# Gate slabs of the second half in pairs, by seven block products in place of eight

## The chip, the cores and the metric

The kernel runs on 1 core of one Trainium2 chip. The metric is the device time of one execution in microseconds. Before the change it is 2825.84 us, the median of 3 runs (2825.59 to 2826.05).

## What is computed

One inference step of a one-layer encoder with two branches, on 2048 prompt rows and 64 sample rows of width 1024, in float32. Cut to the parts that matter here:

```python
h = rmsnorm(x, norm_g)
q, k, v, ga, u, gb, mg = split(h @ w_in)        # six parts of 1024 columns, mg of 2048
att = stick_breaking(q, k, v)                   # 8 heads of 128, strictly causal
p   = trailing_mean(u, windows 2, 4, 8, 16) - u # 4 groups of 256 channels
pb  = (p @ w_pool[group]) * pool_scale
y_a = (att * silu(ga)) @ w_br_a
y_b = (pb  * silu(gb)) @ w_br_b
m   = sigmoid(mg[:, :1024]) * y_a + sigmoid(mg[:, 1024:]) * y_b
y   = rmsnorm(x + m @ w_out, final_g)
```

The sample attends to 4096 cached keys too. New keys, values and the last pooling rows are outputs as well.

## The kernel before

**Products.** Every float32 operand is split exactly into two parts of at most 12 significant bits, `hi` and `lo` (function `split`: a cast on ScalarE, then a subtraction on VectorE). One product of two operands is three matmuls: hi·hi, lo·hi, hi·lo. A contraction over 1024 is eight tiles of 128, so 24 matmuls per block of one PSUM bank.

**Halves.** The rows are worked off in two halves: first prompt rows 0 to 1023 with the 64 sample rows, then prompt rows 1024 to 2047. `hhi` and `hlo` hold the transposed, normalised rows of the half at hand. A *slab* is 128 columns of `w_in`: `proj` loads it (two transfers of 256 KB into `raw`, three buffers), splits it into `whi` and `wlo` (two buffers each), and multiplies it with the half's row blocks (`GROUPS_B`: two blocks of 512 rows in the second half). 48 matmuls make one slab there. An `evac` function then takes the bank.

**Stages of a half.** The heads: projections of a head beside the attention of the head before it. The attention's tail, with gate slabs beside it. Pooling groups (`pool_group`: two slabs of u, window sums on VectorE, a split, and a map of 12 matmuls per block that is deferred, `mapped`) and the other gate slabs: 8 *branch gates* (silu of gb) and 16 *merge gates* (sigmoid of mg). In the first half the attention of the sample runs beside the last two.

A branch gate is stored to DRAM as `gb_d`, loaded again when the pooling needs it (`gbl`), multiplied into the pooled map and stored as `bT_d`. Merge gates are stored to `sm_d`, attention results to `aT_d`.

**Closing.** `load_weight` brings a 1024 x 1024 weight in 16 tiles (`wraw`, split into `bwhi` and `bwlo`), `load_rows` eight row tiles (`rraw`, into `rhi` and `rlo`). `branch` then multiplies, in five blocks of up to 424 rows and eight channel tiles each, first for y_a, then for y_b; the last stage multiplies with w_out. For the first of these, rows and weights are loaded while 15 merge slabs of the second half run, through two raw buffers:

```python
rawp = [wside, 2]
...
raw = rawp[0].tile([P, 512], F32, name="wraw", bufs=rawp[1])
...
early = chain(load_weight(w_br_a[0], wa), load_rows(aT_d, *POST[0], wside, rows0))
run((chain(*[proj(GROUPS_B, [merge_gate(1, c)]) for c in range(1, 2 * KT)]), 15 * slab_ns(1)), (early, 30.0))
```

**What sets the order.** TensorE runs in the order in which the program is traced. `run` takes several generators of steps and traces them spread evenly over one another; `defer` puts a function off by some time, and `settle(True)` traces all that is still put off. On the other engines and on SP, which issues all of these transfers, a scheduler sets the order when the program is built; each then runs strictly in that order.

Of the kernel before, what the change touches and what calls it, by code (L numbers as in the profile page):

```python
# [15 lines left out]
P = 128  # L16
# [16 lines left out]
# rows of a half, as the columns of its transposed operand: blocks of one PSUM bank  # L33
# [4 lines left out]
# rows of the closing phases: prompt 0..1023, sample, prompt 1024..2047  # L38
# [5 lines left out]
def kernel(  # L44
# [18 lines left out]
    gb_d = dram.tile([D, R], F32, name="gb_d")  # L63
# [10 lines left out]
    def split(hi, lo, src, eng=None):  # L74
        """src = hi + lo exactly, each part of at most 12 significant bits."""
        if eng == "v":
            nc.vector.tensor_copy(hi, src)
        else:
            nc.scalar.copy(hi, src)  # L79
        (nc.gpsimd if eng == "g" else nc.vector).tensor_tensor(lo, src, hi.bitcast(F32), op=ALU.subtract)  # L80
# [12 lines left out]
    # row tiles: half A holds prompt rows 0..1023 and the sample, half B the other prompt rows  # L93
# [21 lines left out]
    def run(*gens):  # L115
        """Trace the generators' steps, spread evenly over one another: (generator, its time in ns)"""
# [26 lines left out]
    with ExitStack() as front:  # L143
# [13 lines left out]
        # of the sample's new keys, for two heads: NEG where key >= query; and the identity of 64, twice  # L157
# [104 lines left out]
        def load_w(src, kts, width, eng=None):  # L262
            """src [kts * 128, width] -> hi, lo [128, kts, width]"""
# [33 lines left out]
        def gate_evac(half, dst, row, silu):  # L297
            def evac(g, c0, n, ps):
                s = outgoing("sgm")
                nc.scalar.activation(s[:, 0:n], ps[:, 0:n], AF.Sigmoid)  # L300
                if silu:
                    nc.vector.tensor_tensor(s[:, 0:n], ps[:, 0:n], s[:, 0:n], op=ALU.mult)
                r0 = half * RA + c0
                nc.sync.dma_start(dst[row:row + P, r0:r0 + n], s[:, 0:n])
            return evac

        def merge_gate(half, c):
            return (OFF_M + c * P, gate_evac(half, sm_d, c * P, False))

        def branch_gate(half, c):  # L310
            return (OFF_GB + c * P, gate_evac(half, gb_d, c * P, True))

# [1 line left out]
        def pool_group(half, gi):  # L314
            w = WINDOWS[gi]
            groups = groups_of(half)
            parts, gates = {}, {}
# [7 lines left out]
            def pooled(hi, lo, t0, n, ext, start):  # L325
                """rows whose u lies at columns BUF.. of ext, after its predecessors"""
# [17 lines left out]
            def evac_u(s):  # L344
                c = gi * 2 + s

                def evac(g, c0, n, ps):
# [22 lines left out]
                    if s == 1:  # L370
                        for t in range(2):
                            row, r0 = (gi * 2 + t) * P, half * RA + c0
                            gates[t, g] = attp.tile([P, 528], F32, name="gbl", tag="be", bufs=8)
                            nc.sync.dma_start(gates[t, g][:, 0:n], gb_d[row:row + P, r0:r0 + n])
# [4 lines left out]
            def mapped(g, c0, n, s):  # L379
# [4 lines left out]
                for k in range(2):  # L384
# [10 lines left out]
            # the maps of a block follow the next block's first products  # L395
# [41 lines left out]
        # q, k, gate (transposed) and v (by rows) of the sample  # L437
# [13 lines left out]
        def natural(src, rows, dst):  # L451
            """src [128, rows] transposed to rows, stored at dst [rows, 128]; returns the tile"""
# [12 lines left out]
        def head_proj(half, hd, fine=False):  # L465
# [10 lines left out]
            def spill(kind, c, o, src):  # L476
                """k (transposed) or v (by rows) of the first half's rows, for the second half"""
# [79 lines left out]
        def strictly_causal(t, fill):  # L557
            """t [128 queries, 128 keys]: fill where key >= query"""
# [3 lines left out]
        def weights_of_block(z, off, carry, diag=False, be=None):  # L562
            """z [128, keys] at columns off.. (in PSUM, or in be) -> break weights, and the stick that is left"""
# [23 lines left out]
        class Stream:  # L587
            """The attention of a half's prompt rows: scores of tile n, transposes of tile n - 4,
            products with the values of tile n - 5."""
# [72 lines left out]
            def steps(self, hd):  # L662
                """up to the last score of a head (None: to the end)"""
# [12 lines left out]
        def sample_stream():  # L676
# [5 lines left out]
            def keys(n):  # L682
# [3 lines left out]
                if c == NEW:  # L686
# [7 lines left out]
                    # [hi, lo], [lo, hi]; [hi, 0], [0, hi]  # L694
# [27 lines left out]
            def scores(n):  # L722
# [7 lines left out]
                # each head's bank: the products of q_hi in the head's own rows, that of q_lo in the others  # L730
# [30 lines left out]
            def transposes(n):  # L761
# [7 lines left out]
                # [key, key tile, head, part, query]  # L769
# [289 lines left out]
```

## Time and profile before

| | |
|---|---|
| median of 3 runs | 2825.84 us |
| span of the profiled execution, first to last instruction | 2823.3 us |
| TensorE busy (matmuls) | 2771.4 us, 98% |
| VectorE (DVE) busy | 1678.2 us, 59% |
| ScalarE (ACT) busy | 1194.2 us, 42% |
| GpSimd (POOL) busy | 447.9 us, 16% |
| moved by DMA | 307.83 MB, 109 GB/s on average |
| heads of the first half | until about 570 us |
| attention's tail, sample, pooling and gates of the first half | about 570 to 1110 us |
| heads of the second half | about 1110 to 1820 us |
| attention's tail with four branch gates, second half | about 1820 to 1925 us |
| pooling and the other gates, second half | about 1925 to 2260 us |
| closing phases | from 2260.4 us |

The profile is one execution. Its span runs from the first to the last instruction; the time of a run is some 2.5 us longer. Matmuls are pipelined, so the length of a matmul row is more than the spacing of two matmuls, and TensorE can count as busy in a small gap. In a row of the timeline the first number is the start, the second the length; in brackets stands the idle time of the engine before it and what ended it. In a row of waits stand the waiting engine and tile, what it waited for, the total, the number of waits and the longest. In a row of a stretch stand its bounds and length, the busy time and number of instructions of TensorE, its weight loads, VectorE, ScalarE and GpSimd, then the granted clock of TensorE, the busy share of the DMA engines and GB/s.

### The profile page before, as it was taken

How to read it: one execution, taken by the hardware profiler on the slowest of the kernel's cores; microseconds unless marked ns; L12 is line 12 of the kernel's file. 1: busy time of each engine (PE TensorE's matmuls, PEld its weight loads, DVE VectorE, ACT ScalarE, POOL GpSimd, SP SyncE). 2: the span in 40 equal slices, each digit the busy share in tenths (PEclk: the TensorE clock that was granted, in tenths of full speed). 3: DMA queues.
4: the chain of work that ended last, by engine and by line, in shares of the span. 5: the costliest groups of instructions: out<-in, count | busy, mean ns of one | idle time of the engine just before them, and what ended most of it. 6: DMA issues, size and time to landing. Idle time of an engine off the chain costs nothing.

```text
span 2823.3 us, 42058 instructions
## 1 busy us (share of the span) xinstructions
PE 2771.4 (98%) x15044; PEld 2415.1 (86%) x15044; DVE 1678.2 (59%) x2847; ACT 1194.2 (42%) x2500; POOL 447.9 (16%) x1107
## 2 busy tenths in 40 slices
PE   6999999999999999999999999999999999999998
PEld 5988898889998988888888888887778899999877
DVE  6555555577768683578887888885442022434543
ACT  4445444455555553455555555553223111211221
POOL 2112222220000002233343334330000000000000
PEclk9999999999999999999999999999999999999999
DMA  4223222234444454211111111113344264666432
GB/s 148 73 87 125 71 71 71 84 106 157 151 149 149 155 164 127 72 46 49 57 53 46 49 57 53 34 57 98 116 127 148 75 210 142 214 193 199 162 130 88
DMA packets 333309, 307.83 MB, mean 109 GB/s; under 512 B 30302, under 2 KB 288078, under 8 KB 333100
## 3 DMA queue, kind: packets, MB, share of 16 engines
q1 hardware_dynamic: 333100, 305.15, 34.4%
q8 instruction: 118, 1.93, 0.3%
q14 instruction: 91, 0.75, 0.1%
HBM read 208.99 MB, written 96.07 MB: 108 GB/s over the span
## 4 chain that ended last, share of the span: by engine, by line
PE 93%; DVE 4%; ACT 1%; DMA 1%; issue 1%; POOL 0%; SPq 0%; DVEq 0%; ACTq 0%; POOLq 0%
PE pj L282 17%; PE pj L284 17%; PE pj L283 17%; PE ps L952 4%; PE ps L953 4%; PE ps L954 4%; PE tr L636 4%; PE att L653 2%; PE att L652 2%; PE att L651 2%; PE ps L1015 2%; PE z L625 2%; PE ps L1016 2%; PE ps L1014 2%; PE z L624 2%; PE z L623 2%
## 5 line engine op out<-in xcount | busy, mean ns | idle before, releaser
L282 PE MATMUL pj<-hhi,whi 128*128 128x512 f32 (+2 forms) x2608 | 945.2, 362 | 0.0
L284 PE MATMUL pj<-hhi,wlo 128*128 128x512 f32 (+2 forms) x2608 | 917.9, 352 | 0.5 <-DVE wlo L80 0.5
L283 PE MATMUL pj<-hlo,whi 128*128 128x512 f32 (+2 forms) x2608 | 916.8, 352 | 0.1
L284 PEld LDWEIGHTS pj<-hhi,wlo 128*128 128x128 f32 x2608 | 491.9, 189 | 65.9 <-DVE wlo L80 1.0
L282 PEld LDWEIGHTS pj<-hhi,whi 128*128 128x128 f32 x2608 | 494.4, 190 | 59.6 <-ACT sgm L300 0.4
L283 PEld LDWEIGHTS pj<-hlo,whi 128*128 128x128 f32 x2608 | 493.4, 189 | 58.8 <-DVE hlo L80 0.4
L577 DVE TENSOR_TENSOR_SCAN om<-om 128x513 f32<-128x513 f32 (+3 forms) x356 | 388.0, 1090 | 212.5 <-POOL om L559 108.2
L567 ACT ACTIVATE om<-z 128x512 f32<-128x512 f32 (+2 forms) x320 | 171.3, 535 | 323.0 <-PE z L625 273.9
L80 DVE TENSOR_TENSOR wlo<-raw,whi 128x512 fp32r<-128x512 f32 x248 | 171.6, 696 | 199.8 <-ACT whi L79 198.8
L580 DVE TENSOR_TENSOR be<-be,om 128x512 f32<-128x512 f32 (+3 forms) x356 | 230.4, 647 | 31.4
L79 ACT CAST whi<-raw 128x512 fp32r<-128x512 f32 x256 | 158.1, 623 | 171.4 <-PE pj L283 154.0
L79 ACT CAST a<-tr 128x512 fp32r<-128x512 f32 (+2 forms) x356 | 188.1, 528 | 100.4 <-PE tr L636 89.7
L80 DVE TENSOR_TENSOR a<-tr,a 128x512 fp32r<-128x512 f32 (+2 forms) x356 | 215.8, 607 | 23.8 <-ACT a L79 21.7
L952 PE MATMUL ps<-rhi,bwhi 128*128 128x424 f32 (+1 forms) x640 | 226.7, 354 | 0.8 <-issue 0.8
L953 PE MATMUL ps<-rlo,bwhi 128*128 128x424 f32 (+1 forms) x640 | 226.8, 354 | 0.0
L954 PE MATMUL ps<-rhi,bwlo 128*128 128x424 f32 (+1 forms) x640 | 226.3, 354 | 0.0
L579 POOL COPY carry<-om 128x1 f32<-128x1 f32 x356 | 77.9, 219 | 921.7 <-DVE om L577 881.2
L79 ACT CAST rhi<-rraw 128x424 fp32r<-128x424 f32 (+4 forms) x128 | 66.3, 523 | 293.2 <-PE ps L954 221.6
L956 DVE TENSOR_TENSOR bo<-ps,sg 128x424 f32<-128x424 f32 (+1 forms) x80 | 47.8, 597 | 228.7 <-PE ps L954 216.3
L636 PE MATMUL tr<-ident,be 128*128 128x128 f32 x1088 | 176.0, 274 | 6.1 <-DVE be L580 3.6
L636 PEld LDWEIGHTS tr<-ident,be 128*128 128x128 f32 x1088 | 136.5, 140 | 44.9 <-DVE be L580 8.1
L568 ACT ACTIVATE be<-z 128x512 f32<-128x512 f32 (+2 forms) x320 | 170.1, 532 | 0.0
(180 smaller groups left out, 4111.3 us busy)
## 6 DMA issues: line engine op xcount, KB each, us to landing
raw<-in_w_in_dram SPq DMA_DIRECT2D x256, 256.0 KB, 3.1
kraw<-in_cache_k_dram SPq DMA_DIRECT2D x64, 256.0 KB, 3.5
vraw<-in_cache_v_dram SPq DMA_DIRECT2D x64, 256.0 KB, 2.9
sg<-sm_d SPq DMA_DIRECT2D x64, 212.0 KB, 2.6
sm_d<-sgm SPq DMA_DIRECT2D x48, 256.0 KB, 2.1
out_dram<-nat SPq DMA_DIRECT2D x42, 256.0 KB, 2.3
aT_d<-ao SPq DMA_DIRECT2D x32, 256.0 KB, 2.0
xo<-in_x_prompt_dram SPq DMA_DIRECT2D x16, 512.0 KB, 3.6
```

Source lines behind the costliest of these rows:

```text
L79: nc.scalar.copy(hi, src)
L80: (nc.gpsimd if eng == "g" else nc.vector).tensor_tensor(lo, src, hi.bitcast(F32), op=ALU.subtract)
L282: nc.tensor.matmul(ps[:, 0:n], whi[:, k], hhi[:, k, c0:c0 + n], start=k == 0, stop=False)
L283: nc.tensor.matmul(ps[:, 0:n], whi[:, k], hlo[:, k, c0:c0 + n], start=False, stop=False)
L284: nc.tensor.matmul(ps[:, 0:n], wlo[:, k], hhi[:, k, c0:c0 + n], start=False, stop=k == KT - 1)
L567: nc.scalar.activation(om[:, off:512], z[:, off:512], AF.Sigmoid, scale=-SCALE)
L577: nc.vector.tensor_tensor_scan(rev, rev, rev, 1.0, op0=ALU.mult, op1=ALU.bypass)
L580: nc.vector.tensor_tensor(be[:, off:512], be[:, off:512], om[:, off + 1:513], op=ALU.mult)
L636: nc.tensor.transpose(tr[:, i * P:(i + 1) * P], be[:, off + j * P:off + (j + 1) * P], ident)
L952: nc.tensor.matmul(ps[:, 0:n], whi[:, ws], hi[:, 0:n], start=k == 0, stop=False)
L953: nc.tensor.matmul(ps[:, 0:n], whi[:, ws], lo[:, 0:n], start=False, stop=False)
L954: nc.tensor.matmul(ps[:, 0:n], wlo[:, ws], hi[:, 0:n], start=False, stop=k == KT - 1)
```

## The change

In the second half, 4 of the 24 gate slabs (merge gates 0 to 3) stay as they are and move beside the attention's tail. The other 20 (8 branch gates, 12 merge gates) are taken in pairs of neighbours. Rows in two blocks of 512, contraction in two blocks of 512 and columns in two slabs of 128 make a 2 x 2 block product, which is done by seven block products of 12 matmuls each in place of eight (a scheme of Strassen's kind, in Winograd's form). With a11, a12 (first block of rows), a21, a22 (second) and b11 to b22 alike:

- of the rows: s1 = a21 + a22, s2 = s1 - a11, s4 = a12 - s2 (`row_forms`, traced beside the pooling), s3 = a11 - a21 (`row_forms_last`, written over a21), each split again;
- of the columns, per pair: t1 = b12 - b11, t3 = b22 - b12, t2 = b22 - t1, t4 = b21 - t2 (`col_forms`), and seven splits for four;
- products: one bank `x` takes a11·b11, s2·t2, s3·t3, a22·t4 one after the other and is copied to SBUF three times in between; `y` takes s1·t1, then s4·b22; `z` takes a12·b21. Three additions on VectorE make the results.

The pooled map is scaled on ScalarE (`pbo`) and stored to `bT_d` before the branch gates. A branch gate block loads it (`pbl`), multiplies, and stores it again; `gb_d` is gone. In the first half, merge slabs change places with branch slabs for that. The rows and weights of the first closing phase are traced after the gates, rows first.

```diff
-        def gate_evac(half, dst, row, silu):
...
+        def branch_gate_out(src, row, r0, n):
+            pb = stage("pbl")
+            nc.sync.dma_start(pb[:, 0:n], bT_d[row:row + P, r0:r0 + n])
+            s = outgoing("sgb")
+            nc.scalar.activation(s[:, 0:n], src, AF.Sigmoid)
+            nc.vector.tensor_tensor(s[:, 0:n], src, s[:, 0:n], op=ALU.mult)
+            nc.vector.tensor_tensor(s[:, 0:n], s[:, 0:n], pb[:, 0:n], op=ALU.mult)
+            nc.sync.dma_start(bT_d[row:row + P, r0:r0 + n], s[:, 0:n])
...
-                bt = gates[s, g]
-                nc.vector.scalar_tensor_tensor(bt[:, 0:n], pb[:, 0:n], pscale[:, c:c + 1], bt[:, 0:n],
-                                               op0=ALU.mult, op1=ALU.mult)
+                bt = outgoing("pbo")
+                nc.scalar.activation(bt[:, 0:n], pb[:, 0:n], AF.Identity, scale=pscale[:, c:c + 1])
                 nc.sync.dma_start(bT_d[c * P:(c + 1) * P, r0:r0 + n], bt[:, 0:n])
...
-            rest += [proj(GROUPS_A, [branch_gate(0, c)]) for c in (2 * g, 2 * g + 1) if c > 1]
-            rest.append(proj(GROUPS_A, [merge_gate(0, 3 * g)]))
             rest.append(pool_group(0, g))
-            rest += [proj(GROUPS_A, [merge_gate(0, 3 * g + i)]) for i in (1, 2)]
-        rest += [proj(GROUPS_A, [merge_gate(0, c)]) for c in range(12, 2 * KT - 2)]
+            rest += [proj(GROUPS_A, [merge_gate(0, 2 + 2 * g + i)]) for i in (0, 1)]
+            rest += [proj(GROUPS_A, [branch_gate(0, c)]) for c in (2 * g - 2, 2 * g - 1) if g]
+        rest += [proj(GROUPS_A, [merge_gate(0, c)]) for c in range(10, 2 * KT - 2)]
+        rest += [proj(GROUPS_A, [branch_gate(0, c)]) for c in (6, 7)]
...
-        run((tail_att, tail_ns), (chain(*[proj(GROUPS_B, [branch_gate(1, c)]) for c in range(4)]), 4 * pns))
-        rest = []
-        for g in range(4):
-            rest += [proj(GROUPS_B, [branch_gate(1, c)]) for c in (2 * g, 2 * g + 1) if c > 3]
-            rest.append(pool_group(1, g))
-        rest.append(proj(GROUPS_B, [merge_gate(1, 0)]))
-        run((chain(*rest), 1.0))
+        run((tail_att, tail_ns), (chain(*[proj(GROUPS_B, [merge_gate(1, c)]) for c in range(4)]), 4 * pns))
         settle(True)
         attx.close()
...
+        def stmp(name):
+            return strp.tile([P, 512], F32, name=name, tag="stmp", bufs=8)
...
+        def put(nm, i, src):
+            split(forms[nm][0][:, i], forms[nm][1][:, i], src)
+
+        def row_forms():
+            for i in range(4):
+                r11, r12 = block(nc.gpsimd, i, top, "r11"), block(nc.gpsimd, 4 + i, top, "r12")
+                r21, r22 = block(nc.vector, i, bot, "r21"), block(nc.vector, 4 + i, bot, "r22")
+                nc.vector.tensor_tensor(r21, r21, r22, op=ALU.add)
+                put("s1", i, r21)
+                nc.vector.tensor_tensor(r11, r21, r11, op=ALU.subtract)
+                put("s2", i, r11)
+                nc.vector.tensor_tensor(r12, r12, r11, op=ALU.subtract)
+                put("s4", i, r12)
+                yield 1.0
...
+            for pair in (("b11", "b21"), ("t2", "t1"), ("t3", "b22"), ("t4",)):
+                hi = pool.tile([P, 2, 4, P], F32R, name="fhi", tag="whi", bufs=2)
+                lo = pool.tile([P, 2, 4, P], F32R, name="flo", tag="wlo", bufs=2)
...
+            def product(ps, a, b, first):
+                ahi, alo = forms[a]
+                whi, wlo = w[b]
+                for k in range(4):
+                    nc.tensor.matmul(ps, whi[:, k], ahi[:, k], start=first and k == 0, stop=False, skip_group_check=True)
+                    nc.tensor.matmul(ps, whi[:, k], alo[:, k], start=False, stop=False, skip_group_check=True)
+                    nc.tensor.matmul(ps, wlo[:, k], ahi[:, k], start=False, stop=k == 3, skip_group_check=True)
+                return 12 * mm_ns(512)
...
+            x = psum.tile([P, 512], F32, name="pj")
+            d = product(x, "a11", "b11", True)
+            x1 = kept(x, "x1")
+            yield d
+            z = psum.tile([P, 512], F32, name="z")
+            d = product(z, "a12", "b21", True)
+            nc.vector.tensor_tensor(x1, z, x1, op=ALU.add)
+            emit(0, 0, x1)
+            yield d
+            d = product(x, "s2", "t2", False)
+            x2 = kept(x, "x2")
...
+            d = product(y, "s4", "b22", False)
+            nc.vector.tensor_tensor(x2, y, x2, op=ALU.add)
+            emit(1, 0, x2)
+            yield d
+            d = product(x, "a22", "t4", False)
+            emit(0, 1, x)
+            yield d
...
+        run((chain(*[pool_group(1, g) for g in range(4)]), 8 * pns), (row_forms(), 4.0))
+        settle(True)
+        row_forms_last()
+        run((chain(*[gates(OFF_GB, branch_gate_out, c) for c in range(0, KT, 2)]), 1.0))
+        run((chain(*[gates(OFF_M, merge_gate_out, c) for c in range(4, 2 * KT, 2)]), 1.0))
+        settle(True)
+        strx.close()
         sidex.close()
...
-        early = chain(load_weight(w_br_a[0], wa), load_rows(aT_d, *POST[0], wside, rows0))
-        run((chain(*[proj(GROUPS_B, [merge_gate(1, c)]) for c in range(1, 2 * KT)]), 15 * slab_ns(1)), (early, 30.0))
-        settle(True)
+        run((chain(load_rows(aT_d, *POST[0], wside, rows0), load_weight(w_br_a[0], wa)), 1.0))
```

How the order of the engines moves shows at three places. The first is ScalarE where the first closing weights are cast. Before (`sgm` a merge gate's sigmoid, `whi` a slab's cast, `bwhi` that of a closing weight):

```order
L79 CAST whi<-raw 128x512
L79 CAST bwhi<-wraw 128x512 x2
L300 ACTIVATE sgm<-pj 128x512
L79 CAST bwhi<-wraw 128x512 x4
L300 ACTIVATE sgm<-pj 128x512
L79 CAST whi<-raw 128x512 x2
L79 CAST bwhi<-wraw 128x512 x2
```

Now (`fhi` a column form's cast, the COPY rows are the three banks kept, `rhi` the cast of a row tile; of the first 16 row tiles eight belong to the first block of rows and eight to the second):

```order
L78 CAST fhi<-t_24305 128x512
L966 COPY x_24388<-z 128x512
L966 COPY x_24402<-pj 128x512
L298 ACTIVATE sgm<-x_24402 128x512
L298 ACTIVATE sgm<-x_24373 128x512
L298 ACTIVATE sgm<-pj 128x512
L78 CAST rhi<-rraw 128x424 x16
L78 CAST bwhi<-wraw 128x512 x16
```

The casts of the closing rows and weights moved from among the merge gates to behind the last one.

The second is TensorE at the end of the second half's pooling. Before (`pj_23025` and `pj_23058` are the two blocks of merge slab 0, `z_23071` the last map's bank, `phi_22994` and `plo_22995` the split of the last block of u):

```order
L284 MATMUL pj_23025<-hhi_98,wlo_23016 128x512
L282 MATMUL pj_23058<-hhi_98,whi_23015 128x512
...
L284 MATMUL pj_23058<-hhi_98,wlo_23016 128x512
L386 MATMUL z_23071<-phi_22929,wphi_22792 128x512
L387 MATMUL z_23071<-plo_22930,wphi_22792 128x512
L388 MATMUL z_23071<-phi_22929,wplo_22793 128x512
L386 MATMUL z_23071<-phi_22994,wphi_22792 128x512
```

Now (`pj_22775` is the last block of u itself, `phi_22825` and `plo_22826` its split, `pj_22933` the bank `x` of the first pair):

```order
L283 MATMUL pj_22775<-hhi_97,wlo_22615 128x512
L404 MATMUL tr_22842<-ident_67,hist_90 15x128
L391 MATMUL z_22847<-phi_22758,wphi_22600 128x512
L392 MATMUL z_22847<-plo_22759,wphi_22600 128x512
L393 MATMUL z_22847<-phi_22758,wplo_22601 128x512
L391 MATMUL z_22847<-phi_22825,wphi_22600 128x512
L392 MATMUL z_22847<-plo_22826,wphi_22600 128x512
...
L959 MATMUL pj_22933<-hhi_97,fhi_22911 128x512
```

36 matmuls of a merge slab stood between the last block of u and its map; now a transpose does.

The third is VectorE at the same place, from the block's copy to its split. Before (`wlo` is a slab's split, `s2` to `s16` the window sums):

```order
L80 TENSOR_TENSOR wlo_23110<-raw_23111,whi_23109 128x512
L359 COPY hist_91<-ext_22996 128x15
L331 TENSOR_TENSOR s2_23000<-ext_22996 128x526
L80 TENSOR_TENSOR wlo_23110<-raw_23115,whi_23109 128x512
L331 TENSOR_TENSOR s4_23002<-s2_23000 128x524
L331 TENSOR_TENSOR s8_23004<-s4_23002 128x520
L331 TENSOR_TENSOR s16_23006<-s8_23004 128x512
L340 SCALAR_TENSOR_TENSOR s16_23006<-s16_23006,ext_22996 128x512
L80 TENSOR_TENSOR plo_22995<-s16_23006,phi_22994 128x512
```

Now (`flo_22918` holds the splits of t2 and t1 of the first pair, `t1_23067` is a column form of the second pair):

```order
L79 TENSOR_TENSOR flo_22918<-t2_22907,fhi_22917 128x512
L368 COPY hist_90<-ext_22827 128x15
L340 TENSOR_TENSOR s2_22831<-ext_22827 128x526
L79 TENSOR_TENSOR flo_22918<-t1_22903,fhi_22917 128x512
L340 TENSOR_TENSOR s4_22833<-s2_22831 128x524
L935 TENSOR_TENSOR t1_23067<-b12_23061,b11_23059 128x512
L340 TENSOR_TENSOR s8_22835<-s4_22833 128x520
L340 TENSOR_TENSOR s16_22837<-s8_22835 128x512
L349 SCALAR_TENSOR_TENSOR s16_22837<-s16_22837,ext_22827 128x512
L79 TENSOR_TENSOR plo_22826<-s16_22837,phi_22825 128x512
```

One more operation stands in that chain, a combination of column forms that needs two weight tiles of the second pair.

More of the change, by code (lines that the diff above doesn't have):

```diff
@@ L316, in pool_group @@
             groups = groups_of(half)
-            parts, gates = {}, {}
+            parts = {}
             wraw = pool.tile([P, 2, 256], F32, name="wraw", tag="raw", bufs=3)
@@ L370, in evac @@
                     if s == 1:
[L371 to L374, printed above, removed]
                         defer(8000, lambda: mapped(g, c0, n, 0))
@@ L877 @@
         settle(True)
         attx.close()
+        strx = ExitStack()
+        strp = strx.enter_context(tc.tile_pool(name="strp", bufs=1, side="left"))
+        forms = {nm: [strp.tile([P, 4, 512], F32R, name=f"{nm}{part}") for part in ("hi", "lo")]
+                 for nm in ("s1", "s2", "s4")}
+        top, bot = slice(0, 512), slice(512, 1024)
+        for nm, ks, rs in (("a11", slice(0, 4), top), ("a12", slice(4, 8), top), ("a22", slice(4, 8), bot),
+                           ("s3", slice(0, 4), bot)):
+            forms[nm] = [hhi[:, ks, rs], hlo[:, ks, rs]]
@@ new lines, in stmp, with block @@
+        def stmp(name):
+            return strp.tile([P, 512], F32, name=name, tag="stmp", bufs=8)
+        def block(eng, k, rs, name):
+            t = stmp(name)
+            eng.tensor_tensor(t, hhi[:, k, rs].bitcast(F32), hlo[:, k, rs].bitcast(F32), op=ALU.add)
+            return t
+        def put(nm, i, src):
[11 more added lines that the diff above has]
+                yield 1.0
```

66 lines of the change are left out of this document (56 added, 10 removed).

## The prediction

> **What bounds the kernel now.** I read the page's busy times and its chain first, then the waits of TensorE, then TensorE's own rows in the second half, where the change sits.
>
> ```profile
> span 2823.3 us, 42058 instructions
> PE 2771.4 (98%) x15044; PEld 2415.1 (86%) x15044; DVE 1678.2 (59%) x2847; ACT 1194.2 (42%) x2500; POOL 447.9 (16%) x1107
> PE 93%; DVE 4%; ACT 1%; DMA 1%; issue 1%; POOL 0%; SPq 0%; DVEq 0%; ACTq 0%; POOLq 0%
> ```
>
> TensorE is busy for 98% and carries 93% of the chain that ended last. A busy share may hide small gaps, so the waits from 1820 to 2300 us come next (the attention's tail, pooling, gates, start of the closing phase: the stretch that the change rewrites):
>
> ```profile
> PE tr L636 <- DVE be L580: 1.1, 3, 0.5
> PE ps L952 <- issue: 0.8, 1, 0.8
> ```
>
> Two waits, 1.9 us in 480: TensorE sets the pace, so a matmul taken out there is worth its full spacing, and any new wait of TensorE costs its full length. The spacing is read from starts in the timeline (a row's own 0.39 us is a pipelined length):
>
> ```profile
> 2239.93 0.40 PE L282 MATMUL pj<-hhi,whi 128*128 128x512 f32 x1
> ...
> 2258.74 0.39 PE L282 MATMUL pj<-hhi,whi 128*128 128x512 f32 x1
> 2258.97 0.40 PE L283 MATMUL pj<-hlo,whi 128*128 128x512 f32 x1
> 2259.20 0.40 PE L284 MATMUL pj<-hhi,wlo 128*128 128x512 f32 x1
> 2260.39 0.43 PE L952 MATMUL ps<-rhi,bwhi 128*128 128x424 f32 x1 [0.78 <-issue]
> ```
>
> From the first row to the second are 81 matmuls: 18.81 / 81 = 0.2322 us each. The last gate matmul ends at 2259.60 (I call this moment G), and the closing phase follows at once, because its rows and weights were loaded and split beside the merge gates.
>
> **Term 1, the products.** A pair of slabs was 2 x 2 blocks x 24 = 96 matmuls and becomes 7 x 12 = 84. Ten pairs save 120 matmuls (the instruction order has 13351 rows for 13471): 120 x 0.2322 = **-27.9 us**, since the new matmuls have the same shape and type. The Trainium skill's page "TensorE: Matmul & The Clock Gate", section "Back-to-back issue gap", gives about 131 ns as the sustained spacing at 512 columns. By it the term would be -15.7 and the sum 12 us higher; the trace shows 0.2322 and decides.
>
> **Term 2, the stream of the first closing weights.** Eight row tiles and sixteen weight tiles of the first closing phase used to be interleaved with 15 merge slabs. Now their casts stand on ACT behind the very last sigmoid, and their raw tiles still share two buffers. So the stream runs when TensorE has nothing else. The same stream, same buffers, is in the trace of before (window 2088 to 2160), the weights first:
>
> ```profile
> L892 SPq DMA_DIRECT2D wraw<-in_w_br_a_dram x16: 328/336/604, 2092.0 to 2128.0; - x16
> L79 ACT CAST bwhi<-wraw x16: 620/621/625, 2094.8 to 2130.8; 128x512 fp32r<-128x512 f32 x16
> L80 DVE TENSOR_TENSOR bwlo<-wraw,bwhi x16: 684/693/695, 2095.5 to 2131.7; 128x512 fp32r<-128x512 f32 x16
> DMA to landing us min/median/max: 2.5/3.1/4.9
> ...
> L904 SPq DMA_DIRECT2D rraw<-aT_d x8: 319/338/455, 2130.4 to 2145.6; - x8
> L79 ACT CAST rhi<-rraw x8: 546/547/548, 2134.6 to 2149.3; 128x424 fp32r<-128x424 f32 x8
> L80 DVE TENSOR_TENSOR rlo<-rraw,rhi x8: 593/600/602, 2135.2 to 2149.9; 128x424 fp32r<-128x424 f32 x8
> DMA to landing us min/median/max: 2.3/3.2/4.8
> ```
>
> Sixteen weights took from 2092.0 to 2132.4 (the last split's start plus 0.69), 2.52 us each; eight rows 2130.4 to 2150.5, 2.51 each. That is what two buffers allow: a tile holds its buffer for landing, cast and split, and two take turns.
>
> The first channel tile of the closing phase needs all 8 rows and 8 of the weights, k by k. The first row's DMA stands on SP behind the store of the second-last sigmoid. That follows the end of product 6, which is G minus 12 x 0.2322, by an add (0.69), a sigmoid (0.59) and two issues (0.34 each): about G - 1. Sixteen tiles at 2.52 end at G + 39.3, and with three last matmuls TensorE is through that tile at G + 39.9. Before, it was through at 2260.39 + 24 matmuls. Their spacing is 20 / 105 = 0.19 us by this window row (other lengths in the paragraph are rows below):
>
> ```profile
> 2280.00:2300.00 20.00, 20.00 (x105) 19.47 (x104) 6.71 (x12) 4.38 (x8) 0.00 (x0) 1.00 0.86 292
> L300 ACT ACTIVATE sgm<-pj 128x512 f32<-128x512 f32 x48 | 28.5, 594 | 62.5 <-issue 36.2 <-PE pj L284 26.4
> ```
>
> That is 2264.96, or G + 5.4. The wait: **+34.5 us**. The other eight weights come in 8 x 2.52 = 20 us while four channel tiles take 18; the last k then ends about with them, so I add nothing. Bounds: with the fastest landings, (2.3 + 0.55 + 0.60) / 2 = 1.72 and (2.5 + 0.62 + 0.69) / 2 = 1.90 a tile, the wait is 23; with the slowest (4.8 and 4.9), 2.98 and 3.11 a tile, it is 43. I take the middle: gate traffic on SP is gone, but the next block's rows, gate tiles and 2 MB of inputs now stand between the same DMAs.
>
> **Term 3, the end of the pooling.** The last u block's map had a merge slab as cover; now it is traced right behind that block's last product. The chain to be waited for, in before:
>
> ```profile
> 2077.30 0.39 PE L284 MATMUL pj<-hhi,wlo 128*128 128x512 f32 x1
> 2078.07 0.58 ACT L358 COPY ext<-pj 128x512 f32<-128x512 f32 x1
> 2078.81 0.17 DVE L359 COPY hist<-ext 128x15 f32<-128x15 f32 x1
> 2080.10 2.17 DVE L331 TENSOR_TENSOR s<-s 128x524 f32<-128x524 f32 x3
> 2082.30 0.69 DVE L340 SCALAR_TENSOR_TENSOR s<-s,ext 128x512 f32<-128x512 f32 x1
> 2083.08 0.62 ACT L79 CAST phi<-s 128x512 fp32r<-128x512 f32 x1 [3.48 <-DVE s L340]
> 2083.74 0.69 DVE L80 TENSOR_TENSOR plo<-s,phi 128x512 fp32r<-128x512 f32 x1 [0.74 <-ACT phi L79]
> ```
>
> From the product's end (2077.69) to the split's (2084.43) are 6.74 us, with two weight splits of 0.69 between; now three operations stand between, so 7.43. TensorE covers 1.2 of it (a tail transpose 0.28, four map matmuls): **+6.2 us**. Bounds: 4.2 with nothing between on DVE (6.74 - 2 x 0.69 - 1.2), 10 if one combine there also waits a landing of 3.1.
>
> **Term 4, the clock after a long wait.** The trace has one such case, near the start:
>
> ```profile
> 34.28 0.69 PE L457 MATMUL tr<-ident,kst 128*128 128x128 f32 x2 [5.56 <-DVE hlo L80]
> 34.00:38.00 4.00, 3.72 (x18) 3.73 (x19) 3.90 (x12) 0.75 (x2) 0.97 (x1) 0.50 0.14 39
> 38.00:42.00 4.00, 2.68 (x21) 2.48 (x19) 4.00 (x5) 1.18 (x2) 3.28 (x3) 0.91 0.00 1
> ```
>
> After 5.56 us without work the granted clock was 0.50 for 4 us: 2 us of work lost. Terms 2 and 3 each leave such a gap (three matmuls per 2.5 us is hardly work), so 2 x 2 = **+4 us**; ends 0 and 4.8 (with the 0.91 counted).
>
> **What I cost at nothing, and its cover.** Row forms: 44 DVE operations and 12 adds on POOL, beside the pooling.
>
> ```profile
> L331 DVE TENSOR_TENSOR s<-s x24: 687/694/704, 1955.3 to 2081.6; 128x512 f32<-128x512 f32 x12, 128x516 f32<-128x516 f32 x4, 128x524 f32<-128x524 f32 x4, 128x520 f32<-128x520 f32 x4
> L657 POOL TENSOR_TENSOR ao<-ao,sga 128x512 f32<-128x512 f32 x3 | 4.2, 1415 | 11.1 <-ACT ao L656 11.1
> 880.00:900.00 20.00, 18.97 (x124) 16.97 (x121) 19.45 (x51) 11.39 (x26) 1.98 (x6) 1.00 0.40 129
> ```
>
> Four pool groups are 480 matmuls or 111 us of TensorE; DVE needs 92 + 44 operations of 0.69 = 94 us, POOL 12 x 1.42 = 17. It fits, without much to spare; uncovered, each DVE operation costs 0.69. In a branch pair DVE has 22 operations (4 combines, 7 splits, 3 adds, 8 multiplies), 15.2 us of the pair's 84 x 0.2322 = 19.5; in a merge pair 14. ACT has 15 of about 0.6. A bank that goes on accumulating is copied (0.6) during another product (2.8). DMAs stay equal in number: a gate block stores, loads, stores as before, and a pair still loads four weight tiles; on SP they queue with the pooled map's loads. The map's scaling moves from DVE to ACT, which is busy 42%. In the first half the gates change places with the pooling; the last row above is a stretch of it where DVE was full (19.45 of 20) and TensorE lost 1.0, four such groups exist before and after: 0, ends -2 and +4.
>
> **Sum.** -27.9 + 34.5 + 6.2 + 4.0 = +16.8 on the profiled execution's 2823.3. The median of the runs, 2825.84, lies 2.5 above that span, so I forecast **2842.6 us**.
>
> **Rivals.** *The stream at its fastest.* Idle engines and an empty queue give the shortest landings: wait 23 and the sum +5.3, 2831.1. For it: ACT waited 20.5 us for these DMAs in before, when they shared the queue. Against: 2.3 and 2.5 are minima. On the same case the Trainium skill's "DMA: Bandwidth & Descriptors", section "Anatomy of one DMA — SWDGE (gpsimd) path", fits a transfer as 2.0 us plus its bytes at 436 GB/s. That would be 2.5 and 2.6 us here, an estimate 0.1 to 0.2 above those minima, for another issuing path.
>
> *Faster: bandwidth paces the stream, not the two buffers.* At the 292 GB/s of the window row above, 8 x 217 + 8 x 262 KB take 13.1 us; the tile is through at about G + 14, the wait is 8.6 and the sum -9.1: 2816.7. It decides below 1.1 us a tile (wait under 12). Against: cast plus split alone hold a buffer for 1.15 to 1.31, and landing comes on top.
>
> *DVE paces the pairs.* If each pair waits for one late operation of 0.69 at its head, ten pairs add 6.9: 2849.5. For it: a split waits on ACT's cast, and the second-last add stands before the next pair's first split. Against: 4 us of slack per branch pair.
>
> *The change doesn't do what it says* can be left out: the order shows the products and the 120 matmuls less.
>
> **How the numbers follow.** Forecast 0.68 (its own range 2836 to 2849), DVE-paced pairs 0.12, fastest stream 0.10, bandwidth-paced 0.06, something slower elsewhere 0.04. With 0.2% (5.65 us, about what a measurement here can tell): slower 0.84, same 0.10 (the fastest stream lies at that edge), faster 0.06. All terms at their low ends give about 2823, at their high ends with DVE-paced pairs 2866; the range 2830 to 2856 leaves out both tails.
>
> **What will show it.** Right: a gap of TensorE in front of the closing phase's first tile, broken by threes of matmuls some 2.5 us apart, released by the splits of rows and weights; a gap of 6 us at the last map; pairs of 19.5 us; granted clock near 0.5 after each gap. Wrong: tiles following each other in under 1.5 us, or waits of TensorE at every pair.

## The result, and the profile after

The changed kernel takes 2852.97 us (median of 4 runs, 2851.73 to 2854.79), the kernel before 2825.72 in the same comparison (4 runs, 2823.19 to 2826.05): ratio 1.0099, 95% interval 1.0085 to 1.0114. It is slower by 27.2 us, where 16.8 were forecast. The profiled executions differ by 29.8 us (2853.1 against 2823.3). The page after:

```profile
span 2853.1 us, 42167 instructions
PE 2752.7 (96%) x14924; PEld 2397.6 (84%) x14924; DVE 1780.0 (62%) x2991; ACT 1267.4 (44%) x2626; POOL 472.1 (17%) x1119
PE 89%; DVE 6%; DMA 2%; ACT 1%; issue 1%; SPq 0%; POOL 0%; DVEq 0%; ACTq 0%; POOLq 0%
```

TensorE does 120 matmuls less and is busy 18.7 us less, and yet the span grew: the saving was turned into waits. From 1820 to 2300 us, where before had 1.9 us of them (columns: what TensorE waits to do, for whom, total, times, longest):

```profile
PE ps L1080 <- ACT bwhi L78: 31.2, 6, 20.9
PE tr L404 <- DVE hist L368: 9.6, 3, 7.7
PE z L391 <- ACT phi L78: 4.2, 1, 4.2
PE pj L281 <- ACT ext L367: 2.1, 2, 1.4
PE tr L640 <- DVE be L584: 0.5, 1, 0.5
```

Three places: the start of the closing phase (31.2), the end of the pooling (4.2, with 1.3 of the 9.6 just before it), and the first pooling group (7.7, 1.4 and some smaller ones, together 10). I expected the first two. The third was costed at nothing.

The closing phase. TensorE's timeline after: the last gate matmul, the first closing matmul, and the last two of its first channel tile (24 matmuls):

```profile
2251.06 0.40 PE L961 MATMUL pj<-hhi,flo 128*128 128x512 f32 x1
2272.34 0.69 PE L1080 MATMUL ps<-rhi,bwhi 128*128 128x424 f32 x1 [20.88 <-ACT bwhi L78]
...
2292.47 0.56 PE L1081 MATMUL ps<-rlo,bwhi 128*128 128x424 f32 x1
2292.82 0.56 PE L1082 MATMUL ps<-rhi,bwlo 128*128 128x424 f32 x1
```

The last matmul of the same tile before:

```profile
2264.91 0.35 PE L954 MATMUL ps<-rhi,bwlo 128*128 128x424 f32 x1
```

The last gate matmul ends at 2251.46 (G), and TensorE is through the first channel tile at 2293.38, G + 41.9; before, it was through at 2265.26, G + 5.7. The window rows of that stretch (stretch; its length, then busy time of PE, PEld, DVE, ACT and POOL; granted clock, DMA share, GB/s):

```profile
2250.00:2260.00 10.00, 1.45 (x7) 0.83 (x5) 1.76 (x4) 2.75 (x6) 0.00 (x0) 0.80 0.68 216
2260.00:2270.00 10.00, 0.00 (x0) 0.00 (x0) 6.39 (x11) 5.94 (x11) 0.00 (x0) 0.50 0.91 291
2270.00:2280.00 10.00, 4.30 (x9) 2.37 (x9) 3.25 (x5) 2.45 (x5) 0.00 (x0) 0.50 0.86 276
2280.00:2290.00 10.00, 3.95 (x9) 2.40 (x9) 2.08 (x3) 1.85 (x3) 0.00 (x0) 0.50 0.68 232
2290.00:2300.00 10.00, 9.13 (x33) 8.51 (x34) 3.60 (x6) 3.09 (x5) 0.00 (x0) 0.65 0.54 173
```

The weights' DMAs of the stream (their line, duration of the issue, start of the first and of the last):

```profile
L1022 SPq DMA_DIRECT2D wraw<-in_w_br_a_dram x16: 327/333/907, 2268.0 to 2307.7; - x16
```

The granted clock is 0.50 in all three rows from 2260 to 2290, while matmuls come in small groups, and 0.65 in the row after; the first matmuls of the second channel tile still pay for it. ACT and DVE are far from full. The DMA engines are busy 0.86 to 0.91 from 2260 to 2280, more than I had assumed, so "two buffers" and "bandwidth" both had to be tested.

The end of the pooling: last product of the last u block, first map matmul that had to wait, and the first matmul of the pairs at full clock again:

```profile
2045.93 0.40 PE L283 MATMUL pj<-hhi,wlo 128*128 128x512 f32 x1
...
2052.84 0.80 PE L391 MATMUL z<-phi,wphi 128*128 128x512 f32 x1 [4.22 <-ACT phi L78]
...
2058.24 0.40 PE L959 MATMUL pj<-hhi,fhi 128*128 128x512 f32 x1
```

Without waits, a transpose (0.28) and 16 matmul spacings would have put that last row at 2045.93 + 0.28 + 16 x 0.232 = 2049.92. It stands 8.3 us later: 5.5 of waits, 2.8 of slow clock.

The first pooling group, in the order of time, all engines:

```profile
1949.18 0.62 ACT L78 CAST s1hi<-r 128x512 fp32r<-128x512 f32 x1 [1.36 <-DVE r L905]
1949.22 1.64 POOL L894 TENSOR_TENSOR r<-hhi,hlo 128x512 f32<-128x512 f32 x1 [5.79 <-DVE r L905]
1949.66 1.75 DVE L907 TENSOR_TENSOR r<-r,r 128x512 f32<-128x512 f32 x1
1949.70 0.58 ACT L367 COPY ext<-pj 128x512 f32<-128x512 f32 x1
...
1951.94 0.16 DVE L368 COPY hist<-ext 128x15 f32<-128x15 f32 x1
...
1952.25 0.37 PE L404 MATMUL tr<-ident,hist 128*15 128x128 f32 x1 [7.70 <-DVE hist L368]
```

TensorE waits for `hist`, which waits for `ext` on ACT. That copy stands behind the cast of a row combination (`s1hi`), which waits for DVE. And the DVE operation that overlaps POOL's add takes 1.75 us in place of 0.68. In the window rows DVE is busy for 9.4 to 10 of 10 us, with only 12 to 19 operations:

```profile
1930.00:1940.00 10.00, 8.61 (x38) 6.64 (x37) 10.00 (x12) 2.97 (x5) 6.18 (x4) 1.00 0.20 56
1940.00:1950.00 10.00, 3.85 (x16) 2.51 (x14) 10.00 (x19) 3.76 (x7) 2.37 (x2) 0.94 0.00 0
1950.00:1960.00 10.00, 7.75 (x28) 6.30 (x29) 9.44 (x15) 4.85 (x10) 3.18 (x3) 0.72 0.27 85
```

### The profile page after: what moved, and what is told of

The parts are those of the page before. It is cut to its first block, busy times and chain, and to the rows that moved or that the text cites. A ratio compares the mean times of both kernels' runs of the same rounds, so it can differ in the third digit from the quotient of the medians.

```text
span 2853.1 us, 42167 instructions
## 1 busy us (share of the span) xinstructions
PE 2752.7 (96%) x14924; PEld 2397.6 (84%) x14924; DVE 1780.0 (62%) x2991; ACT 1267.4 (44%) x2626; POOL 472.1 (17%) x1119
## 4 chain that ended last, share of the span: by engine, by line
PE 89%; DVE 6%; DMA 2%; ACT 1%; issue 1%; SPq 0%; POOL 0%; DVEq 0%; ACTq 0%; POOLq 0%
PE pj L281 13%; PE pj L282 13%; PE pj L283 13%; PE ps L1080 4%; PE ps L1081 4%; PE ps L1082 4%; PE tr L640 4%; PE att L657 2%; PE att L656 2%; PE z L629 2%; PE z L628 2%; PE att L655 2%; PE z L627 2%; PE ps L1143 2%; PE ps L1144 2%; PE ps L1142 2%
## 5 line engine op out<-in xcount | busy, mean ns | idle before, releaser
L281 PE MATMUL pj<-hhi,whi 128*128 128x512 f32 (+2 forms) x2288 | 819.5, 358 | 2.1 <-ACT ext L367 2.1
L283 PE MATMUL pj<-hhi,wlo 128*128 128x512 f32 (+2 forms) x2288 | 792.2, 346 | 0.5 <-DVE wlo L79 0.5
L282 PE MATMUL pj<-hlo,whi 128*128 128x512 f32 (+2 forms) x2288 | 790.9, 346 | 0.1
L283 PEld LDWEIGHTS pj<-hhi,wlo 128*128 128x128 f32 x2288 | 432.1, 189 | 51.5 <-DVE wlo L79 1.0
L281 PEld LDWEIGHTS pj<-hhi,whi 128*128 128x128 f32 x2288 | 434.3, 190 | 47.7 <-ACT ext L367 3.0
L282 PEld LDWEIGHTS pj<-hlo,whi 128*128 128x128 f32 x2288 | 433.7, 190 | 44.3 <-DVE hlo L79 0.4
L1080 PE MATMUL ps<-rhi,bwhi 128*128 128x424 f32 (+1 forms) x640 | 230.0, 359 | 31.2 <-ACT bwhi L78 31.2
L79 DVE TENSOR_TENSOR wlo<-raw,whi 128x512 fp32r<-128x512 f32 x208 | 147.4, 713 | 90.2 <-ACT whi L78 89.3
L78 ACT CAST whi<-raw 128x512 fp32r<-128x512 f32 x216 | 133.5, 624 | 98.3 <-PE pj L282 88.9
```

The costliest lines, as they stand in the source:

```text
L281: nc.tensor.matmul(ps[:, 0:n], whi[:, k], hhi[:, k, c0:c0 + n], start=k == 0, stop=False)
L282: nc.tensor.matmul(ps[:, 0:n], whi[:, k], hlo[:, k, c0:c0 + n], start=False, stop=False)
L283: nc.tensor.matmul(ps[:, 0:n], wlo[:, k], hhi[:, k, c0:c0 + n], start=False, stop=k == KT - 1)
L1080: nc.tensor.matmul(ps[:, 0:n], whi[:, ws], hi[:, 0:n], start=k == 0, stop=False)
```

## The experiments

Theory: the 29.8 us between the profiled executions are a saving of 28 to 30 and four costs, each with its own place: first pooling group 12, end of the pooling 8, closing stream 38, first half 1. Rivals, place by place: the DMA engines pace the stream, not the buffers; the pooling groups overfill DVE by themselves; the places share a cause and do not add. Gains are given against the changed kernel's median, 2852.97. The runs of one version lie up to 5 us apart, and the kernel before moved by 1.8 us between the comparisons (2823.92 to 2825.72), so a gain is known to a few us.

**Five buffers for the stream.**

```
-        rawp = [wside, 2]
+        rawp = [wside, 5]
```

> The changed kernel with five raw buffers in place of two for the first closing rows and weights; nothing else differs. Two-buffers theory (a tile holds one of two buffers for landing, cast and split, so 16 tiles take 2.5 us each): with five the landings overlap, the 16 tiles then need the 13 us that 3.8 MB take at 291 GB/s, one landing of 3.6, and a share of the later loads; the wait of 35.5 us falls to 12 to 20 and the time to 2829 to 2837 us. Rival, the DMA engines pace it (busy 0.86 to 0.92 from 2258 to 2280 us, because rows of the next blocks load in between): the same bytes in the same order, so 2850 to 2856 us.

Measured: 2828.64 us (10 runs, 2827.41 to 2831.75), against before 1.0015, 1.0005 to 1.0024; that is just below the lower end of the expectation. One number gives back 24.3 of the 27 us. Its waits from 2240 to 2320 us, and the weights' DMAs (start of the first and the last of the 16):

```profile
PE ps L1080 <- ACT bwhi L78: 10.7, 3, 10.3
```

```profile
L1022 SPq DMA_DIRECT2D wraw<-in_w_br_a_dram x16: 327/328/363, 2257.9 to 2273.1; - x16
```

Sixteen DMAs start within 15.2 us; in the changed kernel it was 39.7 us (2268.0 to 2307.7). The first channel tile is through 18.7 us after G in place of 41.9. So the buffers set the pace, and the rival in its strong form (no change) is out.

**Two buffers, the other loads held back.**

```
     with ExitStack() as back:
+        back.enter_context(tc.issue_after(<eighth weight tile's DMA>))
```

> The changed kernel, two buffers as it has them, but every load of the closing phase that the first channel tile does not need (13 row tiles of later blocks, gain, inputs) is issued only behind the eighth weight tile. Two-buffers theory: the landings fall to the shortest seen (2.3 to 2.6 us), the tiles follow each other at 1.72 and 1.90 us, 29 us for 16 of them; about 10 us are won, 2840 to 2846 us. Rival, DMA engines: 3.8 MB alone take 13 us, about 20 us are won, 2831 to 2836 us. If the other traffic does not matter: 2853.

Measured: 2846.79 us (4 runs, 2846.20 to 2847.22), 6.2 won, a little less than the two-buffers theory said and far less than its rival did. The eight rows now start from 2250.3 to 2262.1:

```profile
L1037 SPq DMA_DIRECT2D rraw<-aT_d x8: 319/320/437, 2250.3 to 2262.1; - x8
```

That is 1.69 us a tile, near the 1.72 that I had given for the fastest stream; the first channel tile is through at G + 32.1. Other traffic is thus worth 9.8 us at that tile (6.2 in the whole time; where the other 3.6 went was not followed), and five buffers in place of two are worth 23.2 there. (The wait of 35.5 and the 8.8 that two of the expectations name come from the end of that tile in the changed kernel, read three matmuls too early.) Both theories hold a part, the buffers the larger one.

**The last four slabs plain, the stream beside them.**

```
-  range(4, 2 * KT, 2) in pairs; free the tiles; load rows and weights
+  range(4, 12, 2) in pairs; free the tiles; slabs 12 to 15 plain, rows and weights beside them
```

The plain slabs read rows of which s3 has already taken the place, so their gates for the second row block differ from the reference's.

> The changed kernel, but the last four merge slabs are computed plainly (eight products each pair, no form of the rows), and the pair's tiles are given back ahead of them, so that rows and weights of the closing phase load beside these slabs, as all of them did before the change. My theory: 24 matmuls more, 24 x 0.2322 = +5.6 us; four slabs are 192 x 0.2322 = 44.6 us of cover for the 40 us of the 16 tiles, so the wait and its slow clock, 38.0 us, go: 2853.0 + 5.6 - 38.0 = 2820.6 us. Rival, the stream is slower beside the slabs' own loads: a wait of up to 6 us stays, 2826 us.

Measured: 2830.20 us (10 runs, 2829.28 to 2832.65): 22.8 won, not 32.4. What is left, in the timeline of ACT and of TensorE (the last gate matmul started at 2257.33):

```profile
2262.01 0.62 ACT L78 CAST bwhi<-wraw 128x512 fp32r<-128x512 f32 x1 [1.67 <-DMA wraw<-in_w_br_a_dram]
2262.53 0.59 ACT L298 ACTIVATE sgm<-pj 128x512 f32<-128x512 f32 x1
...
2263.22 0.69 PE L1082 MATMUL ps<-rhi,bwhi 128*128 128x424 f32 x1 [5.49 <-issue]
```

The last gate's sigmoid stands on ACT behind casts of weights that nobody needs yet and that wait for their DMAs, and the closing phase starts 0.1 us after that sigmoid has read its bank. That the bank is what it waited for is argued from this order; no run tested it.

**No row combinations beside the pooling.**

```
-        run((chain(*[pool_group(1, g) ...]), 8 * pns), (row_forms(), 4.0))
+        run((chain(*[pool_group(1, g) ...]), 8 * pns))
```

> The changed kernel without the row combinations s1, s2 and s4 beside the pooling (the block products use the plain first block in their place, so the gates differ); s3 and everything else stays. My theory of the 10 us of waits in the first pooling group: 44 operations of DVE, their casts on ACT and 8 adds of POOL stand ahead of the evacuations of u; without them the waits and the slow clock behind them go, 12 us: 2841 us. Rival: the pooling groups themselves, now back to back with no gate slab between, overfill DVE; then nothing changes, 2853 us.

Measured: 2840.95 us (4 runs, 2840.21 to 2843.19), 12.0 won, as expected. The run leaves out s1, s2 and s4, which are 32 of the 44 DVE operations and eight of the 12 adds; those of s3 stay. The pooling groups alone do not overfill DVE.

**The row combinations on DVE alone, spread.**

```
-                r11, r12 = block(nc.gpsimd, i, top, "r11"), block(nc.gpsimd, 4 + i, top, "r12")
+                (all four blocks on nc.vector, each kept in program order)
-  (row_forms(), 4.0)
+  (row_forms(), 5.3)
```

> The changed kernel with the row combinations on DVE alone, and each of their four steps issued on DVE only behind what is traced before it (steps at 0, 0.19, 0.38 and 0.57 of the pooling), in place of all as early as possible. My theory: the work fits (11 operations a step, 6.9 us, beside a group's 13 to 22 us of 27.9), only its place was wrong; the time is that of the kernel without row combinations, 2841 us. Rival: average room is not room; the later groups have more operations of their own, and waits of 2 to 8 us stay there, 2843 to 2849 us.

Measured: 2841.10 us (4 runs, 2840.36 to 2842.25), 11.9 won: the whole cost, with the whole work done. It fits. But this run changes two things, engine and place; the next one takes them apart.

**The same 12 adds on DVE, order as the scheduler likes.**

```
-        block(nc.gpsimd, ...)
+        block(nc.vector, ...)        (12 adds; nothing pinned)
```

> The changed kernel with the 12 adds of POOL (r11, r12) done by DVE. Theory of the shared path: in the trace each POOL add of 1.74 us holds the DVE operation beside it to about 1.75 in place of 0.68, so it costs DVE 1.07, and on DVE it costs 0.68: the backlog of the first pooling group falls by 12 x 0.39 = 5 us, 2847 to 2850 us. Rival, DVE's operations simply add up: 12 x 0.68 = 8 us more backlog, 2857 to 2861 us.

Measured: 2841.63 us (4 runs, 2840.12 to 2842.72), 11.3 won, about two to four times what my theory said (3 to 6), and the opposite of the rival. DVE got 12 operations more, and the waits from 1920 to 2060 us are those of the pooling's end plus 1.1 us:

```profile
PE z L391 <- ACT phi L78: 4.2, 1, 4.2
PE tr L404 <- DVE hist L368: 2.4, 2, 1.3
```

So with the adds on DVE the place hardly matters; that they were on POOL did. No run spread them on POOL.

The trace shows one reason for winning more than expected. The copy `ext` that stood behind the third `s1hi` on ACT in the changed kernel (1949.70) now stands ahead of it, at 1939.62: 8.9 us earlier, once the 1.2 us by which this execution is ahead in the attention are taken off. So the 11.3 us hold a changed order on ACT too, and no run parts the two.

The adds could hurt in two ways: by holding DVE, or because DVE waits for their results.

**Idle adds on POOL.**

```
+        for _ in range(3): nc.gpsimd.tensor_tensor(idle, hhi..., hlo..., op=ALU.add)    (x4)
```

> The kernel with all row combinations on DVE (2841.63 us), and 12 adds of the same size on POOL whose result nobody reads, ready at the start of the pooling. Theory of the shared path: they hold DVE for 12 x 1.07 = 13 us, and the waits of the first pooling group come back: 2849 to 2855 us. Rival, only the wait for POOL's results was in the way: nothing waits for these, 2841 us.

Measured: 2856.12 us (4 runs, 2854.82 to 2858.91), 14.5 more than without the idle adds, 1.1 above the expected range. Nobody waits for their results, and in the first pooling group ACT's casts and copies stand in the same order as without them, so it is the holding. TensorE's waits from 1920 to 2060 us are back: 7.5 for `hist` and 6.3 for `ext`. POOL's run of ten adds, three of the DVE operations beside it, and the first ones after it:

```profile
1927.38 16.89 POOL L906 TENSOR_TENSOR idle<-hhi,hlo 128x512 f32<-128x512 f32 x10
...
1936.36 1.75 DVE L79 TENSOR_TENSOR s1lo<-r,s1hi 128x512 fp32r<-128x512 f32 x1
1938.03 1.75 DVE L913 TENSOR_TENSOR r<-r,r 128x512 f32<-128x512 f32 x1
1939.70 1.75 DVE L79 TENSOR_TENSOR s2lo<-r,s2hi 128x512 fp32r<-128x512 f32 x1
...
1944.73 0.16 DVE L368 COPY hist<-ext 128x15 f32<-128x15 f32 x1
1944.81 0.68 DVE L340 TENSOR_TENSOR s<-ext 128x512 f32<-128x512 f32 x1
```

Ten adds of POOL in 16.89 us are 1.69 each, and DVE's operations start 1.67 apart: the two take turns, one operation of each at a time.

**The last maps inside the first pair.**

```
-        settle(True)
         row_forms_last()
```

(and the last block's maps in the banks of `tr`)

> The changed kernel, but the maps of the last u block are traced when they fall due, behind the third product of the first pair (36 matmuls, 8.4 us after the block), and in banks of their own. My theory: their chain of 7.4 us is covered, so the waits of 5.5 us and the 2.8 us of slow clock behind them go: 2853.0 - 8.3 = 2844.7 us. Rival: the chain moves into the pair, since DVE has the last forms and the first pair's splits to do there; then half stays, 2849 us.

Measured: 2845.42 us (4 runs, 2840.89 to 2846.14), 7.6 won against 8.3 expected; TensorE has no wait from 2030 to 2100 us. The profiled execution is the lowest of the four, and in it the closing stream is 2 us shorter as well (through the first channel tile at G + 39.7).

**Eight products in the new order.**

```
-        run((chain(*[gates(OFF_GB, branch_gate_out, c) ...]), 1.0))
+        run((chain(*[proj(GROUPS_B, [branch_gate(1, c)]) for c in range(KT)]), 1.0))
         (merge gates likewise; no row_forms, no row_forms_last)
```

The page meant in the expectation is the Trainium skill's "TensorE: Matmul & The Clock Gate", section "Back-to-back issue gap".

> The changed kernel's order (gates behind the pooling, closing loads behind the gates, pooled map apart), but all gates in eight products and no row combinations: the cost of the new order by itself, with the stream and the end of the pooling. Against the run without row combinations, 2840.95 us, it has 120 matmuls more: 120 x 0.2322 = 27.9, so 2868.8 us. By the page's spacing of 131 ns it would be 15.7 more, 2856.7 us.

Measured: 2834.54 us (6 runs, 2833.28 to 2835.35). My expectation missed by 34 us, because I overlooked what its trace shows (TensorE's only wait at the closing phase, and the weights' DMAs):

```profile
PE ps L1082 <- issue: 0.8, 1, 0.8
```

```profile
L1024 SPq DMA_DIRECT2D wraw<-in_w_br_a_dram x16: 327/330/710, 2155.8 to 2192.8; - x16
```

With no pair using the tiles of the combinations, the stream starts in the midst of the gates, and its 38 us vanish: 2868.8 - 38.0 = 2830.8, 3.7 below the measurement (not followed further). It fits the reason why the stream was late: its buffers lie where the pairs' tiles are. Its gates also size the products: 223.9 us for 960 matmuls (2046.04, the third, to 2269.52, the last, and two more), 0.8 of it a wait. The pairs of the changed kernel take 193.5 us for 840 (2058.24, the fourth, to 2251.06, and three more), 0.2306 each. Difference 30.4, or 29.6 without that wait.

**Three edits together** (five buffers, last maps inside the pair, combinations spread on DVE).

> The changed kernel with three edits of the runs before together: five raw buffers for the first closing tiles, the last maps inside the first pair, the row combinations on DVE alone and spread. If each place costs on its own (my theory), the gains add up: 24.3 (2852.97 - 2828.64), 7.6 (to 2845.42) and 11.9 (to 2841.10), so 2852.97 - 43.8 = 2809.2 us. Rival: they share a cause (the slow clock behind each gap, or DVE's backlog), and the sum falls short by 4 us or more, 2813 to 2820 us.

Measured: 2809.28 us (5 runs, 2807.85 to 2811.10), 0.9946 of before, 0.9934 to 0.9959. The gains of the three single runs add up to this within 0.1 us. They are not known that well, so the 0.1 is luck; but the shortfall of 4 us or more that a shared cause would have left is not there. The costs were separate.

**The same, other loads held.**

> As three_mends, and the loads that the first channel tile does not need are issued behind the eighth weight tile. With five buffers the first tile of the closing phase was through 18.7 us after the last gate matmul; 3.8 MB at 291 GB/s are 13.1 us, and with one landing of 2.5 that is 15.6: about 3 us won, 2806 us. Rival: the held loads then come late for the second block of rows, as in the run with two buffers (8.8 us won at the first tile, 6.2 in all): 2809 us or more.

Measured: 2808.59 us (5 runs, 2808.15 to 2809.61): no difference, and not the 3 us hoped for. With five buffers the first wait stays at 10.1 to 10.3 us whether the later loads are held or not; what ends it was not settled.

**The rows beside the merge pairs.**

```
+        sidex.close()                       (ahead of the merge pairs)
+        rside = tile_pool(name="rside", ...) (raw and split rows; loaded beside the pairs)
-        rawp = [wside, 5]
+        rawp = [wside, 3]                   (weights alone, behind the pairs)
```

> As three_mends_held, and the pooling's tiles are given back ahead of the merge pairs, so that the eight row tiles load beside the pairs; only the weights (three raw buffers) come behind them. Eight weights of 2.6 + 0.62 + 0.69 us over three buffers are 10.4 us, the last one's landing 2.6 behind: first tile through 13 us after the last gate matmul, 2803 us. Rival: the row tiles' casts stand ahead of the pairs' own on ACT or DVE and TensorE waits there; then nothing is won, 2806 us or more.

Measured: 2804.71 us (5 runs, 2803.32 to 2806.38), 0.9929 of before, 0.9916 to 0.9943: against 2803 expected; the fastest version, 20 us under the kernel before and 48 under the changed one, with all ten pairs kept. At the start of the closing phase there is left:

```profile
PE ps L1087 <- ACT bwhi L78: 4.1, 5, 2.5
```

## Why the prediction was right in sign and short by 13 us

Against the profiled execution: 16.8 forecast, 29.8 found. By the medians it is 2842.6 against 2852.97, above the forecast's own range of 2836 to 2849.

- Term 1, the products: -27.9 forecast, about -30 found. The mechanism and the spacing of the trace held (0.2306 in the pairs); the 131 ns of the Trainium skill's page "TensorE: Matmul & The Clock Gate", section "Back-to-back issue gap", would have given -15.7, which no run here shows.
- Terms 2 and 4 at the closing phase: 34.5 + 2 forecast. Found: G + 41.9 against G + 5.7 is 36.3 before rounding; from there to the end of the span are 559.7 us (2853.1 - 2293.4), before 558.0 (2823.3 - 2265.3), which adds 1.7, most of it slow clock: 38.0. The first row's DMA started at G - 1, as worked out. The mechanism was right, and the run with five buffers shows it; but the 2.52 us a tile already held some waiting behind other traffic, as the held loads show (1.69). I took the right number from a row that mixed two causes, and part of that is luck: the eight rows took 17.5 us (2250.5 to 2268.0, 2.2 a tile), the eight weights 24.2 (to the end of their last split at 2292.2, 3.0 a tile), and only their mean is near 2.52.
- Terms 3 and 4 at the pooling's end: 6.2 + 2 forecast, 8.3 in the trace (5.5 of waits, 2.8 of slow clock), 7.6 by the run that removed it.
- The pairs: costed at nothing, and right. No wait of TensorE from 2060 to 2250 us:

```profile
2060.00:2250.00 190.00, 190.00 (x826) 154.65 (x825) 104.11 (x163) 82.46 (x145) 0.00 (x0) 1.00 0.36 115
```

- The row combinations: costed at nothing, and wrong; this is the step that failed. "DVE needs 92 + 44 operations of 0.69 = 94 us, POOL 12 x 1.42 = 17. It fits, without much to spare" adds the two engines as if they ran beside each other. They did not: a POOL add made the DVE operation beside it 1.07 us longer, and all 12 stood in the first 42 us of the pooling (1922.5 to 1964.6), where ACT's queue passed the delay on to the evacuations. 12.0 us by the run without the combinations, 11.3 by the one that only moves the adds.
- The first half, costed at 0 (-2 to +4): found 1.2. The attention's last product, before and after (the last start stands behind the "to"):

```profile
L653 PE MATMUL att<-a,v x9: 274/393/503, 1901.1 to 1920.7; 128*128 128x512 f32 x8, 128*128 128x128 f32 x1
```

```profile
L657 PE MATMUL att<-a,v x9: 274/396/505, 1902.2 to 1921.9; 128*128 128x512 f32 x8, 128*128 128x128 f32 x1
```

The sum found: -30 + 38.0 + 8.3 + 12.0 + 1.2 = 29.5, of 29.8.

The rivals: the fastest stream and the bandwidth-paced stream did not come (TensorE was through at G + 41.9, not at G + 28 or G + 14); the pairs paced by DVE did not either. None of them held what went wrong; only "something slower elsewhere", unnamed and given 0.04, covers it.

## What to carry to other kernels

Work that is moved off the bottleneck keeps its price until its cover is named operation by operation: an average of free time over four groups says nothing on the first one, nor on an in-order queue that passes a delay on. Before a load is moved behind the work that hid it, ask which storage it needs and who holds that until when; here one number of buffers was worth 24 of 27 us. And an elementwise operation given to POOL to relieve DVE must be priced on both engines.

## What the hardware showed that I had not expected

A POOL add of two 128x512 tiles in SBUF and DVE's operations with two inputs in SBUF do not overlap: they take turns, some 1.68 us for one of each (DVE rows of 1.75, 0.68 alone; POOL 1.69, and 1.42 on average in the kernel before). So an add on POOL costs a DVE that has such work waiting 1.07 us, more than the 0.68 of doing it itself, and 12 idle ones cost 14.5 us of the whole kernel. One row goes beyond operations with two inputs: in the changed kernel a DVE copy of 128x15 (`ext<-hist`, at 1938.65) took 1.26 us beside a POOL add, where the same copy takes 0.16 at 1945.79. The Trainium skill's page "SBUF — State Buffer", section "🔬 SBUF: two separate sides", says that DVE and GpSimd share one pair of ports under an exclusive lock, held for a whole instruction, which a DVE operation with two SBUF inputs needs too when the GpSimd operation reads SBUF. The traces agree (1.75 us against 0.68).
